# Hybrid decoder block on one core: a group's small matmuls gathered in two places, and a final norm by square root and one Newton step

## The chip, the cores and the metric

The kernel runs on one core of one Trainium2 chip. The metric is the device time of one execution in microseconds (us). Three timed runs of the kernel before gave 611.32, 611.39 and 611.45, median 611.39. One more execution was taken with the hardware profiler.

## The reference, cut to what matters

The input is 256 tokens of width 1024. One combined projection feeds a Mamba-2 mixer (A) and a causal attention (B); both are projected, merged by gates and added to the residual; a gated FFN with a short convolution follows, and a final RMS norm.

```
def hybrid_layer(x, ...):
    proj = rmsnorm(x, norm1_w) @ w_in
    z, xbc_raw, dt_raw, q, k, v, g_raw = split(proj)
    y_ssd = ssd_mixer(z, xbc_raw, dt_raw, ...)        # 32 heads of 64 in 8 groups, state 128, chunk 128
    y_att = moba_attention(rope(q), rope(k), v)       # 16 heads of 64; 256 tokens are one block: plain causal attention
    merged = g_ssd * (y_ssd @ w_ssd_proj) + g_att * (y_att @ w_att_proj)
    x = x + merged @ w_out
    a, gb = split(rmsnorm(x, norm2_w) @ w_ffn_up)     # 2 x 2816
    return x + (silu(causal_dwconv(a)) * gb) @ w_ffn_down
out = rmsnorm(hybrid_layer(x, ...), norm_f_w)         # rmsnorm(x) = x * rsqrt(mean(x*x) + 1e-6) * w
```

## The kernel before, in words

**Units of weights.** Weights stream in as units of up to 128 partitions x 8 x 256 numbers (1 MB), in the order of the list `seq` (L99 on), on SyncE's DMA queue. `next_unit` (L117) loads three units ahead and splits one unit ahead. A split (`split_unit`, L86) works by halves of 1024 columns: ScalarE writes `hi`, the rounded part in the fp32r type (L93), VectorE writes `lo`, the rest (L94). There are four buffers for `hi` and four for `lo`, so a half is split when the half two units earlier is done with. Each product is three TensorE matmuls: hi by hi, hi by lo, lo by hi. `mm_unit` (L129, lines L148 to L150) has the weights stationary and 256 tokens moving: 48 matmuls of 256 columns for a unit. `mm_tok` (L152, lines L165 to L167) has 128 tokens stationary and 512 weight columns moving: 24 matmuls of 512 columns.

**Groups.** The first half of the kernel is a loop over eight groups g (L544). Each group has the unit products `u_bc`, `u_x`, `u_qk`, `u_z` and, in odd groups, `u_v` (lines L327 to L329), in even groups two units of a gate (`u_gate`, in four quarters of a half unit each, driven as a generator). Between the units stand small matmuls in plain float32:

- `s_cb` (L342): C times B into `pcb` (L345, L346); VectorE masks it into `cb` (L348); ScalarE makes the decay matrices `mx` from `acsB` (L354 to L357); VectorE multiplies `mx` by `cb` (L359).
- `s_xt` (L361): four transposes into `pxt` (L366), and VectorE's `xt` (L368).
- `s_y` (L371): sixteen small products `py` of `mx` and `xt` (L381), then the gate by `zt` (L385, L386) and the squares.
- `s_st` (L390): the column sums `stat` (L200) and the reciprocal root on VectorE (`rms_rstd`, L176); `s_pb` (L393): its broadcast `pb` (L210), then `yn`.
- `a_s` (L402): attention scores `s_ps` (L410) and the softmax; `a_t` (L428): six transposes `pt_ps` (L433); `a_o` (L438): `po` (L447) and `yatt`.

In one group the order before is: `u_bc(g)`, `s_y(g-1)`, `u_x(g)`, `a_s(g-1)`, `u_qk(g)`, `s_cb(g)` with `s_st(g-1)`; then in odd groups `u_v`, `a_t(g-1)`, `u_z`, and `s_xt(g)`, `a_o(g-1)`, `s_pb(g-1)` together; in even groups `u_z`, `a_t(g-1)` with `s_xt(g)`, half of the gate, `a_o(g-1)` with `s_pb(g-1)`, the rest of the gate. So TensorE leaves the big products for small ones five times in a group. After the loop the last group's `s_y`, `a_s`, `s_st`, `a_t`, `s_pb`, `a_o` stand between the four units of the first SSD projection.

**PSUM.** Eight banks: three `mm`, two `at` (scores, transposes of the softmax), two `ss` (`pcb`, `pxt`, `stat`, `pb`), one `acc` (`py`, `po`).

**Who sets the order.** TensorE runs in the order of the program (`manual_schedule` over PE alone). For VectorE, ScalarE and the others a planner, with its own estimate of times, fixes an order beforehand; each engine then takes its instructions strictly in that order, so an instruction that waits holds up those behind it.

**The end.** The down projection (L727 on) runs two halves h of 512 output columns, each over 22 tiles k in units of 4, 4, 4, 4, 4 and 2 tiles; in the last unit, token half c = 0 comes first. For h = 1, VectorE adds the residual (L733), ScalarE squares and sums the row (L658), `rms_rstd` makes the reciprocal root by an integer guess (L183) and three Newton steps (L187, L191), and then ScalarE scales the first 512 columns (L740) and VectorE the last 512 (L742), each with its DMA to the output (L741, L743).

Of the kernel before, what the change touches and what calls it, by code (L numbers as in the profile page):

```python
# [8 lines left out]
F32 = mybir.dt.float32  # L9
# [29 lines left out]
def block_kernel(tc, xtok_d, par_d, nf_d, con_d, rope_d, wdt_d, win_d, wgate_d, bg_d, watt_d, wssd_d, wout_d, wup_d, wdn_d, out_d):  # L39
# [3 lines left out]
    with st:  # L43
# [66 lines left out]
        seq += [(wdn_d[h, :, b : min(b + 8, 2 * NF)], min(8, 2 * NF - b)) for h in range(2) for b in range(0, 2 * NF, 8)]  # L110
        raws, units = [], []

        def load_to(n):
# [35 lines left out]
                    nc.tensor.matmul(ps[m], wh, xl, start=False, stop=False)  # L149
                    nc.tensor.matmul(ps[m], wl, xh, start=False, stop=z)  # L150

        def mm_tok(ps, halves, act, k0, nk, by_token=False, cs=(0, 1)):  # L152


            kt = [(hi, lo, kk) for hi, lo, n in halves for kk in range(0, n, 2)]
            order = [(k, c) for k in range(len(kt)) for c in cs]
            if by_token:
                order.sort(key=lambda x: x[1])
            with tc.manual_schedule(engines=PE_ONLY):
                for k, c in order:  # L160
                    hi, lo, kk = kt[k]
                    wh, wl = (w[:, kk : kk + 2].rearrange("p a b -> p (a b)") for w in (hi, lo))
                    xh, xl = (act[k0 + k][:, i, c * P : c * P + P] for i in range(2))
                    o = ps[c].rearrange("p a b -> p (a b)")
                    nc.tensor.matmul(o, xh, wh, start=(k0 + k == 0), stop=False)  # L165
                    nc.tensor.matmul(o, xh, wl, start=False, stop=False)  # L166
                    nc.tensor.matmul(o, xl, wh, start=False, stop=(k0 + k == nk - 1))  # L167

        def mm_tile():
            return ps_mm.tile([P, 2, T], F32, tag="mm", bufs=3, name="mm")  # L170
# [21 lines left out]

        def rms_stat(sqs, inv_n):

            ps = ps_s.tile([P, 2, T], F32, tag="ss", bufs=2, name="stat")
            jobs = [(sq, ones[:, 0:1]) for sq in sqs]
            with tc.manual_schedule(engines=PE_ONLY):
                for i, (sq, one) in enumerate(jobs):
                    for c in range(2):
                        nc.tensor.matmul(ps[:, 0, c : c + 1], sq[:, c * P : c * P + P], one,  # L200
                                         start=(i == 0 and c == 0), stop=(i == len(jobs) - 1 and c == 1))
# [235 lines left out]

        def a_o(g):  # L438
            pts, vt = S[g]["pt"], S[g]["vt"]
            po = ps_s.tile([P, 2, T], F32, tag="acc", bufs=1, name="po")  # L440
            with tc.manual_schedule(engines=PE_ONLY):
                for c in range(2):
                    for j in range(2):
                        o = po[64 * j : 64 * j + 64, 0, :] if c == 0 else po[64 * j : 64 * j + 64, 0, P:T]
                        rhs = flat(pts[j][:, 0:2]) if c == 0 else pts[j][:, 2]
                        vc = (2 * (g % 2) + j) * 64
                        nc.tensor.matmul(o, vt[:, c, vc : vc + 64], rhs, start=(c == 0), stop=(c == 1))  # L447
            p = new_pair("yatt")
            split_pair(p, po[:, 0, :])
            yatt[g] = p  # L450
# [76 lines left out]
        def u_gate(j):  # L527
# [13 lines left out]
                nc.scalar.activation(gt, gt, AF.Tanh, scale=0.5)  # L541
            yield

        for g in range(NG):  # L544
            if g:
                u_bc(g)
                s_y(g - 1)
                u_x(g)
                a_s(g - 1)
            u_qk(g)  # L550
            if g == 0:
                for c in range(2):
# [12 lines left out]
            elif g % 2:  # L565
                s_cb(g)
                s_st(g - 1)
                u_v(g)
                a_t(g - 1)
                u_z(g)  # L570
                s_xt(g)
                a_o(g - 1)
                s_pb(g - 1)
            else:
                s_cb(g)
                s_st(g - 1)
                u_z(g)
                a_t(g - 1)
                s_xt(g)
                gate = u_gate(g // 2)  # L580
                next(gate)
                next(gate)
                a_o(g - 1)
                s_pb(g - 1)
# [12 lines left out]
        mm_tok(pss, next_unit(), yn, 8, 16)  # L597
        a_o(NG - 1)
        mm_tok(pss, next_unit(), yn, 12, 16, by_token=True)
        st_at.close()  # L600
        ssp_st.close()
# [49 lines left out]
                gated(t1, ps, c, 2 + h)  # L651
                nc.vector.tensor_tensor(m, t1, m, op=ALU.add)

        ss2, ss3 = (late.tile([P, 2, 2], F32, name=n) for n in ("ss2", "ss3"))

        def square_sum(dst, src):
            junk = late.tile([P, 512], F32, tag="junk", bufs=2, name="junk")
            nc.scalar.activation(junk, src, AF.Square, accum_out=dst)  # L658

        xw2 = [None] * KD  # L660

# [62 lines left out]
            act.append(p)  # L724

        rstd3 = late.tile([P, 2], F32, name="rstd3")
        for h in range(2):  # L727
            ps = [mm_tile(), mm_tile()]
            for k0 in range(0, NF, 4):
                mm_tok(ps, next_unit(), act, k0, NF, by_token=(k0 + 4 >= NF))  # L730
            for c in range(2):
                x = half(x2[:, c], h)
                nc.vector.tensor_tensor(x, ps[c].rearrange("p a b -> p (a b)"), x, op=ALU.add)  # L733
                square_sum(ss3[:, c, h : h + 1], x)
                if h == 0:
                    nc.gpsimd.tensor_tensor(x, x, half(nfb, 0), op=ALU.mult)
                else:
                    r = rstd3[:, c : c + 1]
                    rms_rstd(r, ss3[:, c, 0:1], 1.0 / D, more=ss3[:, c, 1:2])
                    nc.scalar.activation(half(x2[:, c], 0), half(x2[:, c], 0), AF.Identity, scale=r)  # L740
                    nc.scalar.dma_start(out_d[:, c, 0:512], half(x2[:, c], 0))  # L741
                    nc.vector.scalar_tensor_tensor(x, x, r, half(nfb, 1), op0=ALU.mult, op1=ALU.mult)  # L742
                    nc.sync.dma_start(out_d[:, c, 512:], x)  # L743


def _layout(i):
# [89 lines left out]
```

## Time and profile before

| | |
|---|---|
| median of three runs | 611.39 us |
| profiled execution: its time, and its span | 611.95 us, 610.1 us |
| TensorE busy with matmuls | 592.4 us |
| VectorE, ScalarE busy | 463.6 us, 358.4 us |
| the eight groups | about 14 to 321 us |
| projections, output projection, FFN up | about 321 to 544 us |
| FFN down and end | about 544 to 610 us |

Busy times are those of the whole span. A matmul's listed duration is its latency; matmuls overlap, so the pace of TensorE is read from the distance between two starts. In the rows of the time order the columns are start, duration, engine, line, operation, tiles and shape, how many are merged, and, in brackets, how long the engine stood idle before and what ended that.

### The profile page before, as it was taken

What the parts mean: (1) busy time and instruction counts of PE and PEld (TensorE: products, weight loads), DVE (VectorE), ACT (ScalarE), POOL (GpSimd) and SP (SyncE); (2) the same over time, 40 slices, a digit from 0 to 9 for tenths busy, and PEclk for the clock granted to TensorE, in tenths of its full rate; (3) what the DMA queues carried; (4) which work ended last, traced back from release to release, by engine and by line L of the source; (5) the groups of instructions that cost most, each with busy time, mean ns of one, the idle gap of its engine ahead of it and who ended that gap; (6) DMA issues with size and microseconds to landing.
All of it is one profiled execution on the core that took longest, in us unless ns stands there. A gap on an engine that the chain in (4) does not pass through costs nothing.

```text
span 610.1 us, 10606 instructions
## 1 busy us (share of the span) xinstructions
PE 592.4 (97%) x4194; PEld 543.0 (89%) x4194; DVE 463.6 (76%) x896; ACT 358.4 (59%) x648; POOL 4.1 (1%) x8
## 2 busy tenths in 40 slices
PE   7997999999999999999999999999999999999994
PEld 7996999989999899998988788889999999998883
DVE  5866798968979699796986546667988888884643
ACT  6646867649586495865945334456655555654431
POOL 0000000000000000000000000000000000000100
PEclk9999999999999999999999999999999999999998
DMA  8667265464534545445352755645446455455511
GB/s 330 228 250 271 102 212 173 156 218 136 195 138 172 210 151 182 138 162 208 122 197 102 260 202 192 206 153 193 162 185 205 155 193 196 160 198 179 200 35 69
DMA packets 17746, 109.78 MB, mean 180 GB/s; under 512 B 2176, under 2 KB 2592, under 8 KB 5664
## 3 DMA queue, kind: packets, MB, share of 16 engines
q1 hardware_dynamic: 15120, 100.15, 46.6%
q10 hardware_dynamic: 2576, 8.95, 4.3%
q8 instruction: 33, 0.54, 0.3%
q14 instruction: 17, 0.14, 0.1%
HBM read 107.49 MB, written 1.08 MB: 178 GB/s over the span
## 4 chain that ended last, share of the span: by engine, by line
PE 92%; ACT 3%; DMA 2%; DVE 2%; issue 1%; ACTq 0%; DVEq 0%
PE mm L148 16%; PE mm L149 16%; PE mm L150 16%; PE mm L165 11%; PE mm L167 10%; PE mm L166 10%; PE py L381 2%; PE mm L328 1%; PE mm L327 1%; PE mm L329 1%; DMA acsB<-acsT_d 1%; PE s_ps L410 1%; PE po L447 1%; PE pt_ps L433 1%; ACT hi L93 1%; PE pb L210 1%
## 5 line engine op out<-in xcount | busy, mean ns | idle before, releaser
L93 ACT ACTIVATE hi<-raw 128x1024 fp32r<-128x1024 f32 x186 | 196.0, 1060 | 179.3 <-PE mm L167 79.4
L94 DVE TENSOR_TENSOR lo<-raw,hi 128x1024 fp32r<-128x1024 f32 x186 | 226.7, 1226 | 89.3 <-ACT hi L93 89.0
L148 PE MATMUL mm<-hn,hi 128*128 128x256 f32 x512 | 147.4, 288 | 0.0
L149 PE MATMUL mm<-hn,hi 128*128 128x256 f32 x512 | 145.0, 283 | 0.4 <-DVE hn L220 0.4
L150 PE MATMUL mm<-hn,lo 128*128 128x256 f32 x512 | 144.8, 283 | 0.0
L148 PEld LDWEIGHTS mm<-hn,hi 128*128 128x128 f32 x512 | 98.0, 191 | 4.1 <-issue 3.9
L148 PE MATMUL mm<-xw,hi 128*128 128x256 f32 x352 | 99.8, 283 | 0.0
L149 PE MATMUL mm<-xw,hi 128*128 128x256 f32 x352 | 99.6, 283 | 0.0
L150 PE MATMUL mm<-xw,lo 128*128 128x256 f32 x352 | 99.6, 283 | 0.0
L149 PEld LDWEIGHTS mm<-hn,hi 128*128 128x128 f32 x512 | 98.2, 192 | 0.9 <-DVE hn L220 0.8
L150 PEld LDWEIGHTS mm<-hn,lo 128*128 128x128 f32 x512 | 98.1, 192 | 0.0
L149 PEld LDWEIGHTS mm<-xw,hi 128*128 128x128 f32 x352 | 67.6, 192 | 0.0
L148 PEld LDWEIGHTS mm<-xw,hi 128*128 128x128 f32 x352 | 67.6, 192 | 0.0
L150 PEld LDWEIGHTS mm<-xw,lo 128*128 128x128 f32 x352 | 67.6, 192 | 0.0
L272 DVE SCALAR_TENSOR_TENSOR cacc<-mm,par,cacc 128x255 f32<-128x255 f32 (+2 forms) x96 | 44.2, 475 | 3.0 <-ACT cacc L268 2.9
L165 PE MATMUL mm<-hi,act 128*128 128x512 f32 x88 | 34.2, 389 | 0.0
L166 PE MATMUL mm<-lo,act 128*128 128x512 f32 x88 | 34.2, 389 | 0.0
L167 PE MATMUL mm<-hi,act 128*128 128x512 f32 x88 | 34.2, 389 | 0.0
L166 PE MATMUL mm<-lo,hn 128*128 128x512 f32 x64 | 25.0, 391 | 1.7 <-DVE lo L94 1.7
L165 PE MATMUL mm<-hi,hn 128*128 128x512 f32 x64 | 25.8, 404 | 0.0
L165 PE MATMUL mm<-hi,yn 128*128 128x512 f32 x64 | 25.3, 396 | 0.0
L167 PE MATMUL mm<-hi,hn 128*128 128x512 f32 x64 | 25.0, 391 | 0.0
(170 smaller groups left out, 935.4 us busy)
## 6 DMA issues: line engine op xcount, KB each, us to landing
raw<-in_win_dram SPq DMA_DIRECT2D x35, 1024.0 KB
raw<-in_wup_dram SPq DMA_DIRECT2D x22, 1024.0 KB
raw<-in_wdn_dram SPq DMA_DIRECT2D x10, 1024.0 KB
raw<-in_wgate_dram SPq DMA_DIRECT2D x8, 1024.0 KB
raw<-in_wssd_dram SPq DMA_DIRECT2D x8, 1024.0 KB
acsB<-acsT_d ACTq DMA_DIRECT2D x8, 512.0 KB
raw<-in_watt_dram SPq DMA_DIRECT2D x4, 1024.0 KB
raw<-in_wout_dram SPq DMA_DIRECT2D x4, 1024.0 KB
```

Of the source, the lines that this page charges most:

```text
L93: nc.scalar.activation(hi[:, :n], raw[:, k0 : k0 + n], AF.Copy)
L94: nc.vector.tensor_tensor(lo[:, :n], raw[:, k0 : k0 + n], hi[:, :n].bitcast(F32), op=ALU.subtract)
L148: nc.tensor.matmul(ps[m], wh, xh, start=a, stop=False)
L149: nc.tensor.matmul(ps[m], wh, xl, start=False, stop=False)
L150: nc.tensor.matmul(ps[m], wl, xh, start=False, stop=z)
L165: nc.tensor.matmul(o, xh, wh, start=(k0 + k == 0), stop=False)
L166: nc.tensor.matmul(o, xh, wl, start=False, stop=False)
L167: nc.tensor.matmul(o, xl, wh, start=False, stop=(k0 + k == nk - 1))
L210: nc.tensor.matmul(pb[:, 0, c * P : c * P + P], y[:, c : c + 1].to_broadcast([P, P]), ident, start=True, stop=True)
L272: nc.vector.scalar_tensor_tensor(acc[:, s:], src[:, m, : T - s], w(m, 3 - s), acc[:, s:], op0=ALU.mult, op1=ALU.add)
L327: nc.tensor.matmul(ps[:, c, :], xh, hi[:, kk], start=(k == 0 and c == 0), stop=False)
L381: nc.tensor.matmul(o, xt[:, c, r, :], rhs, start=(c == 0), stop=(c == 1))
```

## The change

Three things are edited.

First, the small matmuls of a group stand in two places, and the end of the attention (`a_o`, with `s_pb`) a group and a half behind its group's units. `small_1(g)` comes after `u_x(g)`: `s_y(g-1)`, `a_s(g-1)`, `a_o(g-2)`, `s_pb(g-2)`. `small_2(g)` comes after the last unit of an odd group and after the third quarter of the gate in an even group: `s_cb(g)`, `s_xt(g)`, `s_st(g-1)`, `a_t(g-1)`. `stat` and `po` swap their PSUM banks. After the loop `small_1(8)` follows `small_2(7)` with no unit between.

Second, the final norm of token half c takes a square root on ScalarE, a reciprocal and one Newton step on VectorE, and a `Sqrt` of one column is put after the last FFN activation.

Third, in the down projection the units become 2, 4, 4, 4, 4, 4 tiles; in the last unit of h = 1, token half 0 is finished first, and token half 1 in two pieces of 256 columns, each added and squared by itself. This end is issued in program order on TensorE, ScalarE and VectorE.

```diff
+IN_ORDER = {mybir.EngineType.PE, mybir.EngineType.Activation, mybir.EngineType.DVE}
...
+        DOWN = ((0, 2), (2, 6), (6, 10), (10, 14), (14, 18), (18, 22))
...
-            ps = ps_s.tile([P, 2, T], F32, tag="ss", bufs=2, name="stat")
+            ps = ps_s.tile([P, 2, T], F32, tag="acc", bufs=1, name="stat")
...
-            po = ps_s.tile([P, 2, T], F32, tag="acc", bufs=1, name="po")
+            po = ps_s.tile([P, 2, T], F32, tag="ss", bufs=2, name="po")
...
+        def small_1(g):
+            if 0 <= g - 1 < NG:
+                s_y(g - 1)
+                a_s(g - 1)
+            if 0 <= g - 2:
+                a_o(g - 2)
+                s_pb(g - 2)
+
+        def small_2(g):
+            if g < NG:
+                s_cb(g)
+                s_xt(g)
+            if 0 <= g - 1:
+                s_st(g - 1)
+                a_t(g - 1)
...
                 u_bc(g)
-                s_y(g - 1)
                 u_x(g)
-                a_s(g - 1)
+                small_1(g)
             u_qk(g)
...
-                s_cb(g)
-                next(gate)
-                s_xt(g)
                 next(gate)
                 next(gate)
+                small_2(g)
+                next(gate)
             elif g % 2:
-                s_cb(g)
-                s_st(g - 1)
                 u_v(g)
-                a_t(g - 1)
                 u_z(g)
-                s_xt(g)
-                a_o(g - 1)
-                s_pb(g - 1)
+                small_2(g)
...
-        s_y(NG - 1)
-        a_s(NG - 1)
+        small_1(NG)
         pss = [mm_tile(), mm_tile()]
         mm_tok(pss, next_unit(), yn, 0, 16)
-        s_st(NG - 1)
+        small_2(NG)
         mm_tok(pss, next_unit(), yn, 4, 16)
-        a_t(NG - 1)
         s_pb(NG - 1)
+        a_o(NG - 1)
         mm_tok(pss, next_unit(), yn, 8, 16)
-        a_o(NG - 1)
         mm_tok(pss, next_unit(), yn, 12, 16, by_token=True)
...
+        nc.scalar.activation(root[:, 0:1], th[:, 0:1], AF.Sqrt, scale=0.0, bias=eps)
...
+        def root3(c, n):
+            nc.scalar.activation(root[:, c : c + 1], ss3[:, c, n - 1 : n], AF.Sqrt, scale=1.0 / D, bias=fin[:, c, 0:1])
+
+        def rstd_3(c, n):
+
+            mh, h, r = (fin[:, c, i : i + 1] for i in (1, 2, 3))
+            nc.vector.scalar_tensor_tensor(h, ss3[:, c, n - 1 : n], -0.5 / D, mh, op0=ALU.mult, op1=ALU.add)
+            nc.vector.reciprocal(r, root[:, c : c + 1])
+            nc.vector.scalar_tensor_tensor(h, r, r, h, op0=ALU.mult, op1=ALU.mult)
+            nc.vector.scalar_tensor_tensor(rstd3[:, c : c + 1], h, 1.5, r, op0=ALU.add, op1=ALU.mult)
...
+        with tc.manual_schedule(engines=IN_ORDER):
+            for a in (0, 256):
+                mm_tok(ps, hv, act, k0, NF, cs=(1,), cols=slice(a, a + 256))
+            mean3(0, 2)
+            add_x3(ps, 1, 0)
+            root3(0, 2)
+            add_x3(ps, 1, 1, 0, 0, 256)
+            rstd_3(0, 2)
+            out_lo(0)
+            mean3(1, 3)
+            add_x3(ps, 1, 1, 1, 256, 512)
+            root3(1, 3)
+            out_hi(0)
+            rstd_3(1, 3)
+            out_lo(1)
+            out_hi(1)
```

`mean3` makes the part of the mean square that is known before the last piece (two to four operations on one column); `add_x3` adds the residual on VectorE and squares and sums on ScalarE; `out_lo` scales on ScalarE and issues the output's DMA on ScalarE's queue; `out_hi` scales on VectorE and issues on SyncE's.

More of the change, by code (lines that the diff above doesn't have):

```diff
@@ L109, in block_kernel @@
         seq += [(wup_d[f], KD) for f in range(NF)]
[L110 removed]
+        DOWN = ((0, 2), (2, 6), (6, 10), (10, 14), (14, 18), (18, 22))
+        seq += [(wdn_d[h, :, 2 * a : 2 * b], 2 * (b - a)) for h in range(2) for a, b in DOWN]
         raws, units = [], []
@@ L161, in mm_tok @@
                     hi, lo, kk = kt[k]
-                    wh, wl = (w[:, kk : kk + 2].rearrange("p a b -> p (a b)") for w in (hi, lo))
+                    wh, wl = (w[:, kk : kk + 2].rearrange("p a b -> p (a b)")[:, cols] for w in (hi, lo))
                     xh, xl = (act[k0 + k][:, i, c * P : c * P + P] for i in range(2))
-                    o = ps[c].rearrange("p a b -> p (a b)")
+                    o = ps[c].rearrange("p a b -> p (a b)")[:, cols]
                     nc.tensor.matmul(o, xh, wh, start=(k0 + k == 0), stop=False)
                     nc.tensor.matmul(o, xh, wl, start=False, stop=False)
-                    nc.tensor.matmul(o, xl, wh, start=False, stop=(k0 + k == nk - 1))
+                    nc.tensor.matmul(o, xl, wh, start=False, stop=(k0 + k == nk - 1 and cols.stop == 512))
         def mm_tile():
@@ L582, in block_kernel @@
                 next(gate)
-                a_o(g - 1)
-                s_pb(g - 1)
+                small_2(g)
                 next(gate)
@@ L652, in block_kernel @@
                 nc.vector.tensor_tensor(m, t1, m, op=ALU.add)
-        ss2, ss3 = (late.tile([P, 2, 2], F32, name=n) for n in ("ss2", "ss3"))
+        ss2 = late.tile([P, 2, 2], F32, name="ss2")
         def square_sum(dst, src):
             junk = late.tile([P, 512], F32, tag="junk", bufs=2, name="junk")
-            nc.scalar.activation(junk, src, AF.Square, accum_out=dst)
+            nc.scalar.activation(junk[:, : src.shape[1]], src, AF.Square, accum_out=dst)
         xw2 = [None] * KD
@@ L726, in block_kernel, with add_x3 @@
         rstd3 = late.tile([P, 2], F32, name="rstd3")
+        ss3 = late.tile([P, 2, 4], F32, name="ss3")
+        eps = late.tile([P, 1], F32, name="eps")
+        nc.vector.memset(eps, EPS)
+        root = late.tile([P, 2], F32, name="root")
+        nc.scalar.activation(root[:, 0:1], th[:, 0:1], AF.Sqrt, scale=0.0, bias=eps)
+        def add_x3(ps, h, c, i=0, a=0, b=512):
+            x = half(x2[:, c], h)[:, a:b]
+            nc.vector.tensor_tensor(x, flat(ps[c])[:, a:b], x, op=ALU.add)
+            square_sum(ss3[:, c, h + i : h + i + 1], x)
@@ new lines, in block_kernel, with mean3 @@
+        fin = late.tile([P, 2, 4], F32, name="fin")
+        def mean3(c, n):
+            m, mh = fin[:, c, 0:1], fin[:, c, 1:2]
+            nc.vector.tensor_scalar(m, ss3[:, c, 0:1], 1.0 / D, EPS, op0=ALU.mult, op1=ALU.add)
+            for i in range(1, n - 1):
+                nc.vector.scalar_tensor_tensor(m, ss3[:, c, i : i + 1], 1.0 / D, m, op0=ALU.mult, op1=ALU.add)
+            nc.vector.tensor_scalar(mh, m, -0.5, None, op0=ALU.mult)
+        def root3(c, n):
+            nc.scalar.activation(root[:, c : c + 1], ss3[:, c, n - 1 : n], AF.Sqrt, scale=1.0 / D, bias=fin[:, c, 0:1])
@@ new lines, in rstd_3, with out_lo @@
+        def rstd_3(c, n):
[4 more added lines that the diff above has]
+            nc.vector.scalar_tensor_tensor(rstd3[:, c : c + 1], h, 1.5, r, op0=ALU.add, op1=ALU.mult)
+        def out_lo(c):
+            x = half(x2[:, c], 0)
+            nc.scalar.activation(x, x, AF.Identity, scale=rstd3[:, c : c + 1])
+            nc.scalar.dma_start(out_d[:, c, 0:512], x)
@@ L727, in block_kernel, with out_hi @@
+        def out_hi(c):
+            x = half(x2[:, c], 1)
+            nc.vector.scalar_tensor_tensor(x, x, rstd3[:, c : c + 1], half(nfb, 1), op0=ALU.mult, op1=ALU.mult)
+            nc.sync.dma_start(out_d[:, c, 512:], x)
         for h in range(2):
             ps = [mm_tile(), mm_tile()]
[L729 to L735, printed above, removed]
-                    nc.gpsimd.tensor_tensor(x, x, half(nfb, 0), op=ALU.mult)
[L737 to L743, printed above, removed]
@@ new lines, in block_kernel @@
+            for k0, _ in DOWN[:-1]:
+                mm_tok(ps, next_unit(), act, k0, NF)
+            hv, k0 = next_unit(), DOWN[-1][0]
+            mm_tok(ps, hv, act, k0, NF, cs=(0,))
+            if h == 0:
+                add_x3(ps, h, 0)
+                mm_tok(ps, hv, act, k0, NF, cs=(1,))
+                add_x3(ps, h, 1)
+                for c in range(2):
+                    x = half(x2[:, c], 0)
+                    nc.gpsimd.tensor_tensor(x, x, half(nfb, 0), op=ALU.mult)
+        with tc.manual_schedule(engines=IN_ORDER):
[14 more added lines that the diff above has]
+            out_hi(1)
```

6 lines of the change are left out of this document (1 added, 5 removed).

## The prediction

> **What bounds the kernel now.** I read the page first, then the stretches, then TensorE's waits.
>
> ```profile
> span 610.1 us, 10606 instructions
> PE 592.4 (97%) x4194; PEld 543.0 (89%) x4194; DVE 463.6 (76%) x896; ACT 358.4 (59%) x648; POOL 4.1 (1%) x8
> ```
>
> ```profile
> 212.20:287.60 75.40, 75.40 (x589) 70.13 (x588) 63.16 (x136) 52.60 (x107) 0.00 (x0) 1.00 0.50 169
> 603.00:610.10 7.10, 0.00 (x0) 0.00 (x0) 2.93 (x15) 1.44 (x2) 0.00 (x0) 0.64 0.39 149
> ```
>
> ```profile
> PE mm L166 <- DVE lo L94: 1.7, 1, 1.7
> PE py L381 <- DVE mx L359: 1.7, 1, 1.7
> PE py L381 <- DVE yatt L174: 1.4, 1, 1.4
> ```
>
> The stretches have, after their bounds and length, the busy time of TensorE, its weight loads, VectorE, ScalarE and GpSimd, the granted clock, the DMA share and GB/s; the waits have their total, number and longest. TensorE is the bound: in two middle groups (75.40 us) it is busy all the time at full clock, VectorE 84% of it. Time can come out in three ways: fewer seams in TensorE's stream, the three waits above (4.8 us in all), and the end after the last matmul. A gain under 0.2% of 611.4, which is 1.2 us, could not be told from no change.
>
> **Part 1: the seams.** The distance between starts is what an instruction costs TensorE.
>
> ```profile
> 136.50 0.28 PE L149 MATMUL mm<-hn,hi 128*128 128x256 f32 x1
> 136.62 0.28 PE L150 MATMUL mm<-hn,lo 128*128 128x256 f32 x1
> 136.83 1.52 PE L381 MATMUL py<-mx,xt 128*64 128x256 f32 x16
> 138.28 0.39 PE L148 MATMUL mm<-hn,hi 128*128 128x256 f32 x1
> 138.50 0.28 PE L149 MATMUL mm<-hn,hi 128*128 128x256 f32 x1
> ...
> 150.94 0.59 PE L345 MATMUL pcb<-bc 128*128 128x256 f32 x2
> ...
> 151.59 0.50 PE L200 MATMUL stat<-ones,zt 128*128 128x1 f32 x4
> 151.96 0.36 PE L327 MATMUL mm<-hi,hn 128*128 128x256 f32 x1
> 152.16 0.28 PE L328 MATMUL mm<-lo,hn 128*128 128x256 f32 x1
> ```
>
> A 256-column matmul follows another after 0.12 us (136.50 to 136.62), so a unit of 48 takes 5.76. Into `py`, which fills half the array, the step is 0.21, and out of it the first big matmul takes 0.22 instead of 0.12: 0.19 lost. Out of `stat` it is 0.20: 0.08 lost. The whole price in a group comes from the chain of waits:
>
> ```profile
> 212.31 1.45 PE py L381 x16
> 247.40 1.45 PE py L381 x16
> ```
>
> From `py` to `py` through an odd group are 35.09 us; five units are 28.80; so the small matmuls with their seams cost 6.29. What they cost back to back is seen at the end of the loop, where they stand together already:
>
> ```profile
> 315.02 0.60 PE L366 MATMUL pxt<-con,xs 128*128 128x128 f32 x4
> 315.54 0.87 PE L447 MATMUL po<-pt,vt 128*64 128x256 f32 x8
> 316.35 0.71 PE L210 MATMUL pb<-con,ry 128*128 128x128 f32 x4
> 318.46 1.52 PE L381 MATMUL py<-mx,xt 128*64 128x256 f32 x16 [1.41 <-DVE yatt L174]
> 319.91 0.93 PE L410 MATMUL s_ps<-qk 64*128 64x128 f32 x8
> 320.77 0.50 PE L165 MATMUL mm<-hi,yn 128*128 128x512 f32 x1
> ...
> 332.25 0.82 PE L433 MATMUL pt_ps<-con,pr 128*128 128x128 f32 x6
> 332.91 0.61 PE L210 MATMUL pb<-con,ry 128*128 128x128 f32 x4
> 333.27 0.48 PE L165 MATMUL mm<-hi,yn 128*128 128x512 f32 x1
> ```
>
> First place: entry 0.09, `py` 1.45, `s_ps` 0.86, `po` 0.81, `pb` 0.36, exit 0.08 to 0.10: 3.66. Second place: `pcb` 0.65, `pxt` 0.44 to 0.52 (0.52 holds an entry into `po`), `stat` 0.37, `pt_ps` up to 0.66, exit 0.08: 2.1 to 2.3. Together 5.8 to 5.9 against 6.29: 0.35 to 0.5 saved in a group. The loop has seven such groups: 2.5 to 3.5. At worst the switch from one kind of small matmul to the next costs as much as a seam, and nothing is saved. I take **-3.2**, since each piece has its own row.
>
> **Part 2: the two waits of the first groups.**
>
> ```profile
> 46.13 0.69 DVE L368 TENSOR_TENSOR xt<-pxt,dt 128x512 f32<-128x512 f32 x1 [1.91 <-PE pxt L366]
> 46.74 4.62 DVE L94 TENSOR_TENSOR lo<-raw,hi 128x1024 fp32r<-128x1024 f32 x4
> ...
> 59.11 1.76 DVE L359 TENSOR_TENSOR mx<-mx,cb 128x1536 f32<-128x1536 f32 x1 [2.68 <-ACT mx L357]
> ```
>
> In the first group VectorE stood idle for `pxt` with four `lo` queued behind `xt`, and TensorE missed the first: 1.7. Now `pxt` comes a quarter of the gate later, behind the matmuls that need this `lo`, so `lo` must come first. The other wait: `py(0)` stood for the `mx` product, which ended at 60.87. `py(0)` now has `u_x(1)`, 5.76 us, ahead of it; 1.7 goes, and the `mx` product, bound by a DMA and ScalarE, is late no more. Next late would be the second `lo` of the gate's last quarter, behind `xt` as before. Between 0 and -3.4; I take **-2.5**.
>
> **Part 3: the end of the loop.** `small_1(8)` follows `small_2(7)` directly, so `py(7)` needs what has just been started. From the start of `pcb`, VectorE must wait some 0.85 (estimate: `pcb` 0.65 and a hand-over), then `cb` (about 0.55, three quarters of the 0.69 of `xt`), `mx` 1.76 and `xt` 0.69: 3.7 at best, with a `lo` of 1.16 and the gate's `zt` (0.69 as `xt`) ahead, 5.5. TensorE has 2.2 us of work until then. It waits 1.5 to 3.3, where it now stands 1.75 (318.46 less 316.35 and 0.36). So -0.2 to +1.6; I take **+0.8**.
>
> **Part 4: the end.**
>
> ```profile
> 600.72 0.39 PE L166 MATMUL mm<-lo,act 128*128 128x512 f32 x1
> 600.94 0.39 PE L167 MATMUL mm<-hi,act 128*128 128x512 f32 x1
> 601.37 0.69 DVE L733 TENSOR_TENSOR x<-mm,x 128x512 f32<-128x512 f32 x1 [0.67 <-PE mm L167]
> 602.09 0.63 ACT L658 ACTIVATE junk<-x 128x512 f32<-128x512 f32 x1 [0.64 <-DVE x L733]
> 602.63 0.19 ACT L658 ACTIVATION_READ_ACCUMULATOR junk<-x 128x1 f32 x1
> 604.87 0.22 DVE L187 SCALAR_TENSOR_TENSOR ra<-rstd,rh 128x1 f32<-128x1 f32 x1
> 605.12 0.16 DVE L191 SCALAR_TENSOR_TENSOR rstd<-ra,rstd 128x1 f32<-128x1 f32 x1
> 605.38 0.72 ACT L740 ACTIVATE x<-x,rstd 128x512 f32<-128x512 f32 x1 [0.84 <-DVE rstd L191]
> 606.13 0.36 ACTq L741 DMA_DIRECT2D out_dram<-x  x1
> ```
>
> From the last add (601.37) to the last scaling (605.38) are 4.01 us: add and square 1.45, the rest the integer guess and Newton chain, each pair of steps about 0.45. Afterwards the last piece is 256 columns. Counted from TensorE's end: VectorE is held about 0.2 by the first token half's root steps; the add takes about 0.42 (between half and all of 0.69); ScalarE is free at 0.84, because `out_lo(0)` with its 0.72 and the DMA issue's 0.36 stand ahead of the square in program order; square and read about 0.52; the one-column root 0.2 to 0.4 (between the read of 0.19 and the 0.63 square), taken 0.3; then reciprocal and two steps at 0.2 to 0.25 each: scaling starts at about 2.4. That saves 1.6. Against it TensorE's last unit: 24 matmuls at 0.12 are 2.88, where twelve at 0.22 to 0.23 take 2.72: +0.16. The output DMA behind it stays. Ends: -2.0 if ScalarE is not held, -0.7 if the dependent steps cost double. I take **-1.4**.
>
> **The cover of part 1.** It is a saving only if nobody comes too late in the new order. The tightest distance is now two units (11.5 us): from `pcb` to the next `py`, and from `stat` to its `pb`. In between VectorE owes `cb` (0.55), the `mx` product (1.76), `xt` (0.69) and the root's dozen steps of 0.2 to 0.25, some 5.7 us, beside four `lo` of 1.16. It fits, and `hi` and `lo` run a unit ahead. The new bank neighbours (`stat` behind `py`, `po` behind `pcb` and `pxt`) were read two units earlier. Taken at nothing; without that cover it is the first rival.
>
> **The table.** The `Sqrt` needs another one. The trace shows one load:
>
> ```profile
> 0.73 1.28 ACT L66 ACT_TABLE_LOAD   x1 [0.73 <-PEq L824]
> ```
>
> A second of 1.28 would come as the down projection starts; ScalarE is idle for 41% of the span and runs a unit ahead: hidden, and 1.28 if not. The Trainium skill (ScalarE: Activation LUTs, section "What ACT_TABLE_LOAD costs") gives 1283 ns, as the row has, and adds a drain of 1380 ns to each switch, which no row here shows; by 2.66 us it would be hidden too.
>
> **Sum.** -3.2 - 2.5 + 0.8 - 1.4 = -6.3. The profiled execution took 611.95 (span 610.1 and 1.85 around it): 605.65. It lay 0.56 above the median of the runs, so **605.1**.
>
> **The rivals.**
>
> *A new convoy on VectorE (slower).* The small places now hand VectorE four things at once. The row at 46.13 shows what happens when the planner puts one that must wait ahead of `lo`: 1.7 us of TensorE. If `py`'s readers or `xt` do that once in each of seven groups, 11.9 come on top: 617.0. From 0.9 us per group the gain of 6.3 is gone. For it: VectorE is 84% busy. Against it: TensorE waits nowhere for over 0.2 us between 62 and 315 us with the same work and the same planner. 10%.
>
> *The first groups wait as before*, `xt` merely blocking another `lo`, and `py(0)` waiting because ScalarE is given `mx` later: 607.6. The planner's estimates failed there once already. 16%.
>
> *The seams are not saved*: each change of kind inside a place costs as much as a seam, so part 1 does not do what it says: 608.3. Against it the back-to-back rows. 12%.
>
> *The tables alternate in the end.* If `Square` and `Sqrt` did not share a table, three loads of 1.28 would fall between the squares and the roots on ScalarE's path, some of the first hidden: about +3.4, 608.5. The Trainium skill (same page, "Table sets: the hidden batching unit") says to batch by set and names relu, copy, identity and abs as common to all sets, not square, which would give just this. 4%.
>
> *Two of the last three together*: about 611. 4%.
>
> **How the numbers follow.** The forecast has 54%. Faster: the forecast and the three middle rivals, 86%; within 0.2%: 4%; slower: 10%. The range goes from 602.8 (parts 2 and 4 near their best ends) to 609.0 (the fourth rival and a little), and leaves out the convoy and the pairs.
>
> **What would show it.** TensorE should leave the big products twice in a group; from `py` to `py` in an odd group should be about 34.6 instead of 35.09; the waits at 48 and 61 us should be gone; at the loop's end one wait of 1.5 to 3.3 before `py`; from TensorE's end to the last scaling about 2.4; two table loads, the second as the down projection starts. New waits of TensorE on `lo` or `mx` between 62 and 310 us, more than two loads, or a distance of 35 or more from `py` to `py` would prove me wrong.

## The result, and the profile after

The changed kernel is slower: median 618.93 us (618.07 to 620.94), beside 611.36 for the kernel before on the same chip; the ratio is 1.0121, with a 95% interval of 1.0102 to 1.0139. The forecast was 605.1, within 602.8 to 609.0. The profiled execution took 618.93 us, its span 617.1. (The ratio is not taken from the two medians and can differ a little from their quotient.)

The page of the changed kernel, with the busy times and the granted clock in forty slices:

```profile
span 617.1 us, 10666 instructions
PE 596.1 (97%) x4206; PEld 549.1 (89%) x4206; DVE 461.9 (75%) x891; ACT 359.3 (58%) x654; POOL 3.9 (1%) x8
PEclk8999989999999999999988999999999999999998
```

VectorE and ScalarE have about as much to do as before (461.9 and 359.3 us busy, where it was 463.6 and 358.4). What is new is in the clock row: it falls at the start, in the sixth slice (77 to 93 us) and in the two slices from 309 to 339 us. The waits of TensorE name the later places, one for the sixth slice and two for the pair:

```profile
PE mm L330 <- DVE lo L95: 3.7, 1, 3.7
PE py L383 <- DVE rv L182: 3.1, 1, 3.1
PE pb L212 <- DVE ry L193: 2.0, 1, 2.0
```

The three waits of before (1.7, 1.7, 1.4) are gone but for 0.3, and these three of 8.8 us have come. To see where the 7.0 us of span lie, both runs are cut at the same matmuls: the first small matmul behind the units of group 1, the one behind the units of group 7, the broadcast of the second norm's factor as the FFN begins, the end. First the kernel before, then the changed one (bounds, length, then busy time of TensorE, its weight loads, VectorE, ScalarE and GpSimd, then granted clock, DMA share, GB/s):

```profile
0.00:88.80 88.80, 81.24 (x629) 75.75 (x630) 66.15 (x150) 55.92 (x109) 1.19 (x6) 1.00 0.64 232
88.80:315.02 226.22, 226.22 (x1767) 210.41 (x1766) 190.20 (x409) 157.56 (x321) 0.00 (x0) 1.00 0.49 170
315.02:422.79 107.77, 106.36 (x553) 88.97 (x552) 70.18 (x120) 52.32 (x81) 0.00 (x0) 1.00 0.54 186
422.79:610.10 187.31, 178.54 (x1254) 167.90 (x1252) 137.09 (x218) 92.60 (x137) 2.92 (x2) 0.99 0.47 163
```

```profile
0.00:90.03 90.03, 82.70 (x615) 77.42 (x615) 62.98 (x136) 55.29 (x107) 1.19 (x6) 0.96 0.63 231
90.03:313.59 223.56, 223.56 (x1767) 210.03 (x1765) 186.33 (x406) 155.64 (x321) 0.00 (x0) 1.00 0.48 169
313.59:429.82 116.23, 111.09 (x567) 92.97 (x565) 76.38 (x139) 53.22 (x83) 0.00 (x0) 0.97 0.52 177
429.82:617.10 187.28, 178.69 (x1266) 168.64 (x1264) 136.25 (x212) 95.14 (x143) 2.75 (x2) 0.99 0.47 163
```

The six middle groups, the body of the change, are 2.66 us shorter, 0.44 a group. The end is as long as before. The loss stands in the first and the third stretch. `pcb`, `stat` and `pt_ps` of one group with their seams (0.65, 0.37, 0.66 and 0.08, together 1.76 us) stood ahead of both cuts and now stand behind them, so they have moved from the first stretch to the third; with that, the first stretch has lost 3.0 and the third 6.7. Of the 3.0, 1.48 lie at the very start: TensorE's clock is at half from 8.6 to 12.0 us, and the first `ps_dt` starts at 20.37 instead of 18.89. That is not the change's doing: of three kernels below that have the loop of before unchanged, the profiles of two show this window and that of the third does not. So 1.5, -2.7, 6.7 and 0 are to be explained.

**The first groups.** ScalarE, then VectorE, then TensorE of the changed kernel, in order of time:

```profile
49.84 0.35 ACTq L301 DMA_DIRECT2D acsB<-acsT_d  x1
...
57.45 0.69 ACT L356 ACTIVATE mx<-acsB,acs 128x128 f32<-128x128 f32 x2 [2.75 <-DMA acsB<-acsT_d]
```

```profile
54.73 1.23 DVE L95 TENSOR_TENSOR lo<-raw,hi 128x1024 fp32r<-128x1024 f32 x1 [0.40 <-ACT hi L94]
62.05 1.76 DVE L361 TENSOR_TENSOR mx<-mx,cb 128x1536 f32<-128x1536 f32 x1 [6.10 <-ACT mx L359]
...
75.89 1.22 DVE L95 TENSOR_TENSOR lo<-raw,hi 128x1024 fp32r<-128x1024 f32 x1
```

```profile
77.17 0.58 PE L330 MATMUL mm<-lo,hn 128*128 128x256 f32 x1 [3.70 <-DVE lo L95]
77.55 0.41 PE L331 MATMUL mm<-hi,hn 128*128 128x256 f32 x1
...
80.32 0.28 PE L329 MATMUL mm<-hi,hn 128*128 128x256 f32 x1
80.44 0.28 PE L330 MATMUL mm<-lo,hn 128*128 128x256 f32 x1
```

The load of `acsB(0)` takes 7.6 us from its issue. ScalarE has the decay matrices of group 0 at the head of its order and waits for it; VectorE has their product at the head of its order and stands idle for 6.10. Everything behind, the convolution of group 1 and the splits, comes late, and `u_v(1)` is the unit that finds no `lo`: 3.7 us. Then, up to 80.32, the steps are 0.21 instead of 0.12: half clock, 1.5 us more (3.15 us for 14 steps of 0.12).

**The end of the loop.** TensorE, then VectorE:

```profile
313.59 0.59 PE L347 MATMUL pcb<-bc 128*128 128x256 f32 x2
...
315.04 0.85 PE L435 MATMUL pt_ps<-con,pr 128*128 128x128 f32 x6
319.01 2.65 PE L383 MATMUL py<-mx,xt 128*64 128x256 f32 x16 [3.12 <-DVE rv L182]
...
325.83 1.04 PE L212 MATMUL pb<-con,ry 128*128 128x128 f32 x4 [2.02 <-DVE ry L193]
327.09 0.63 PE L168 MATMUL mm<-lo,yn 128*128 128x512 f32 x1
328.37 0.63 PE L168 MATMUL mm<-lo,yn 128*128 128x512 f32 x1
```

```profile
313.13 0.69 DVE L317 TENSOR_TENSOR swap<-swap,rope 128x512 f32<-128x512 f32 x1 [1.65 <-DMA swap<-qkraw]
...
316.53 1.75 DVE L361 TENSOR_TENSOR mx<-mx,cb 128x1536 f32<-128x1536 f32 x1
318.20 0.69 DVE L370 TENSOR_TENSOR xt<-pxt,dt 128x512 f32<-128x512 f32 x1
318.80 0.15 DVE L182 TENSOR_SCALAR rv<-stat 128x2 f32<-128x2 f32 x1
...
325.62 0.16 DVE L193 SCALAR_TENSOR_TENSOR ry<-ra,ry 128x2 f32<-128x2 f32 x1
```

`py(7)` needs `mx`, `xt` and the bank from which `rv` reads `stat`; VectorE has them one behind the other, after a swap that waited 1.65 for its DMA, so the wait is called `rv` but is the queue ahead of it. `pb(6)` waits again, for a root chain whose dozen steps VectorE has mixed with splits and softmax: `stat` stands at 314.68, `ry` at 325.62. `py` takes 2.65 instead of 1.52, and between the last two rows three matmuls take 1.28 instead of 0.68: half clock. The visit costs 13.07 us (the distance between the big matmuls around it, less their own step), where a pair of visits in the middle costs 5.89.

**The end.**

```profile
608.23 0.28 PE L169 MATMUL mm<-hi,act 128*128 128x256 f32 x1
608.55 0.42 DVE L742 TENSOR_TENSOR x<-mm,x 128x256 f32<-128x256 f32 x1 [2.18 <-PE mm L169]
...
612.38 0.72 ACT L768 ACTIVATE x<-x,rstd 128x512 f32<-128x512 f32 x1 [0.74 <-DVE rstd L764]
```

The addition of the first piece could start some 1.4 us before TensorE's end; it starts 0.04 after it. From TensorE's end (608.51) to the last scaling are 3.87 us; before they were 4.05 (601.33 to 605.38).

**The theories.** Mine: three separate places, each to be mended by itself, while the middle of the loop brings what was forecast. The rival: an overload of VectorE, or the clock, that shows in these places by chance and would turn up elsewhere.

### The profile page after: what moved, and what is told of

It is laid out like the page before. It is cut to its first block, busy times and chain, and to the rows that moved or that the text cites. A ratio compares the mean times of both kernels' runs of the same rounds, so it can differ in the third digit from the quotient of the medians.

```text
span 617.1 us, 10666 instructions
## 1 busy us (share of the span) xinstructions
PE 596.1 (97%) x4206; PEld 549.1 (89%) x4206; DVE 461.9 (75%) x891; ACT 359.3 (58%) x654; POOL 3.9 (1%) x8
## 4 chain that ended last, share of the span: by engine, by line
PE 87%; ACT 5%; DVE 3%; DMA 3%; issue 1%; ACTq 0%; DVEq 0%
PE mm L151 15%; PE mm L150 15%; PE mm L152 15%; PE mm L168 10%; PE mm L167 10%; PE mm L169 10%; PE py L383 2%; ACT hi L94 1%; DMA acsB<-acsT_d 1%; PE mm L330 1%; PE mm L331 1%; ACT mx L356 1%; PE mm L329 1%; PE s_ps L412 1%; PE pb L212 1%
## 5 line engine op out<-in xcount | busy, mean ns | idle before, releaser
L274 DVE SCALAR_TENSOR_TENSOR cacc<-mm,par,cacc 128x253 f32<-128x253 f32 (+2 forms) x96 | 44.3, 477 | 2.1 <-ACT cacc L270 1.6
L168 PE MATMUL mm<-lo,act 128*128 128x512 f32 (+1 forms) x92 | 35.0, 380 | 0.0
L167 PE MATMUL mm<-hi,act 128*128 128x512 f32 (+1 forms) x92 | 34.9, 380 | 0.0
L169 PE MATMUL mm<-hi,act 128*128 128x512 f32 (+1 forms) x92 | 34.9, 380 | 0.0
L167 PE MATMUL mm<-hi,yn 128*128 128x512 f32 x64 | 25.9, 404 | 0.0
L167 PE MATMUL mm<-hi,hn 128*128 128x512 f32 x64 | 25.5, 399 | 0.0
L168 PE MATMUL mm<-lo,yn 128*128 128x512 f32 x64 | 25.4, 397 | 0.0
L169 PE MATMUL mm<-hi,yn 128*128 128x512 f32 x64 | 25.4, 397 | 0.0
```

The source lines that it names most:

```text
L274: nc.vector.scalar_tensor_tensor(acc[:, s:], src[:, m, : T - s], w(m, 3 - s), acc[:, s:], op0=ALU.mult, op1=ALU.add)
```

## The experiments

Each is compared with runs of the kernel before on the same chip (611.37 to 611.40).

### The new end alone

The kernel before, with only the second and third edit of the change (the diff's core stands in the section on the change).

```diff
+        DOWN = ((0, 2), (2, 6), (6, 10), (10, 14), (14, 18), (18, 22))
...
+        nc.scalar.activation(root[:, 0:1], th[:, 0:1], AF.Sqrt, scale=0.0, bias=eps)
...
+            for a in (0, 256):
+                mm_tok(ps, hv, act, k0, NF, cs=(1,), cols=slice(a, a + 256))
```

> The kernel before with the new end alone: its loop, the places of its small matmuls and its buffers are as they were; only the final rms by square root and one Newton step, the sums by halves and the outputs' order are changed. Theory A (three separate places: the two calls that meet at the end of the loop, the first group's late decay product, and an end whose first half is let go only with the second): the new end gives nothing by itself, 611.4 us within 0.5, and from TensorE's last product to the end of the last scaling it takes about 3.9 us, as in the changed kernel (3.87). Theory B (the new end itself is dear, by a table load or by its longer chain): 613 us or more, and the rest of the loss would then lie in it. The prediction's own figure for the end would give 610.0.

Measured: 610.99 us, ratio 0.9997 (0.9986 to 1.0007); 3.87 us from TensorE's last product (602.49) to the last scaling (606.36). The new end costs nothing and brings nothing that can be told from zero. Its table is loaded behind the last FFN activation (in the changed kernel at 555.39, the second of two loads), and TensorE waits for nothing there.

### The two calls apart

```diff
                 u_v(g)
+                if g == NG - 1:
+                    small_2(g)
                 u_z(g)
-                small_2(g)
+                if g < NG - 1:
+                    small_2(g)
```

> The changed kernel, but in the last group the second call of the small matmuls stands behind the unit of v and ahead of the unit of z, so that the unit of z (about 14 us) lies between it and the next first call. Theory A: the waits of 3.1 us (for rv) and 2.0 us (for ry) at the loop's end go or fall under 0.5 us together, and the half-speed windows behind them with them: 5 to 6.7 us less than the changed kernel, 612.2 to 613.9 us. Theory B (VectorE is loaded too evenly in every group, and the end of the loop only shows what has piled up; or the clock alone): the waits turn up elsewhere, and it stays above 616.9 us.

Measured: 613.02 us, ratio 1.0033 (1.0017 to 1.0049): 5.9 us less than the changed kernel. TensorE:

```profile
315.98 1.52 PE L383 MATMUL py<-mx,xt 128*64 128x256 f32 x16
...
321.40 0.71 PE L212 MATMUL pb<-con,ry 128*128 128x128 f32 x4 [2.25 <-DVE ry L193]
```

The wait before `py` is gone, and no half-clock window is left here. The wait at `pb` stays, which the theory had not expected: from `stat` (309.08) to `pb` are only one unit and the calls' own matmuls, and the root chain needs more.

### The last piece whole

```diff
-            for a in (0, 256):
-                mm_tok(ps, hv, act, k0, NF, cs=(1,), cols=slice(a, a + 256))
+            mm_tok(ps, hv, act, k0, NF, cs=(1,))
...
-            add_x3(ps, 1, 1, 0, 0, 256)
...
-            add_x3(ps, 1, 1, 1, 256, 512)
+            add_x3(ps, 1, 1)
```

> The changed kernel, but the second half of the tokens in the last unit goes in one piece of 512 columns instead of two pieces of 256, its addition, squares, root and Newton step too; the first half's scaling and output stand between. Theory A (the first piece of 256 was released no earlier than the second, so cutting bought nothing and cost 0.16 us on TensorE and two more links on VectorE): from TensorE's last product to the end of the last scaling about 2.6 us instead of 3.87, and 617.5 us in all, 1.4 less than the changed kernel. Theory B (the end is set by the outputs' transfers, or by the table): no change within 0.4 us, 618.5 to 619.3.

Measured: 616.43 us, ratio 1.0075 (1.0054 to 1.0096), 2.5 us less. From TensorE's last product (607.68) to the last scaling (610.45) are 2.77 us, 1.1 less than in two pieces. The rest is mainly the clock (cut as above, the profile is 1.25 us shorter in the last stretch, 2.5 shorter at the loop's end and 1.8 longer in the first groups), and this makes the run worth more than it was meant for. Its loop is that of the changed kernel, and the waits at the loop's end are as long:

```profile
320.74 1.52 PE L383 MATMUL py<-mx,xt 128*64 128x256 f32 x16 [3.03 <-DVE rv L182]
...
326.76 0.71 PE L212 MATMUL pb<-con,ry 128*128 128x128 f32 x4 [2.85 <-DVE ry L193]
...
327.54 0.40 PE L168 MATMUL mm<-lo,yn 128*128 128x512 f32 x1
327.77 0.39 PE L169 MATMUL mm<-hi,yn 128*128 128x512 f32 x1
```

But here the clock stays full behind them (at 77 us its half-speed window is twice as long instead): `py` in 1.52, steps of 0.23 behind. The visit costs 11.91, which is 5.88 of waits and 6.03 of work; the changed kernel's 13.07 are 5.14 of waits, 5.89 of work and 2.0 of half clock, with another 1.1 in the unit behind. So the waits are the larger part and the half clock follows them or not.

### The decay product behind the convolution

`s_cb(0)` without its activations and product, which are called behind `u_bc(1)` and held there in the order of both engines:

```diff
+            if g:
+                s_mx(g)
...
                 u_bc(g)
+                if g == 1:
+                    s_mx(0)
+                    load_acs(1)
```

> The changed kernel, but the decay product of group 0 (twelve activations, the common exponential and VectorE's product) is called behind the unit of B and C of group 1 and held there in the order of ScalarE and VectorE, so that the three splits and the convolutions of group 1 stand ahead of it while it waits for its transfer. Theory A: the 3.7 us wait for lo at about 77 us and the half-speed window behind it go: 3.7 to 5 us less than the changed kernel, 613.9 to 615.2 us, unless the product is then late for its own reader (py of group 0, about 90 us), which would give a wait of 1 us or more there. Theory B (the wait at 77 us comes from too much work on VectorE ahead of it, not from the transfer): a wait of 3 us or more remains before the matmuls of v, and the time stays within 1 us of 618.9.

Measured: 623.6 us, ratio 1.0191 (1.0167 to 1.0216), 4.7 more. The wait for `lo` went, as expected, and the wait that had been named as a reservation came, at eight times the size. VectorE and TensorE:

```profile
71.53 1.76 DVE L370 TENSOR_TENSOR mx<-mx,cb 128x1536 f32<-128x1536 f32 x1 [3.64 <-ACT mx L368]
```

```profile
73.34 2.83 PE L394 MATMUL py<-mx,xt 128*64 128x256 f32 x16 [8.03 <-DVE mx L370]
```

A queue in strict order has one head: putting the late thing behind the others makes it later by all of them. The order was not the fault to mend; the lateness was.

### The broadcast earlier

```diff
+                dt_turn()
+                load_acs(0)
                 gate = u_gate(0)
                 next(gate)
-                dt_turn()
-                load_acs(0)
```

> The changed kernel, but the turn of the running sums and the load of group 0's broadcast (acsB) stand ahead of the first quarter of the gate unit instead of behind it. In the run with the decay product behind the convolution the wait for lo went and a wait of 8.0 us for the product came, so the order of the two only chooses which one is late. Theory A (both are late because the broadcast lands late): landing about 4 us earlier, the product is done before the splits need the engines, the wait at 77 us (3.7 to 4.3 us in three runs) falls under 1 us with no wait for the product in its place, less up to 1 us of a new wait of TensorE for the running sums at 40 us: 613.9 to 616 us. Theory B (ScalarE and VectorE have too much work there, whatever the transfer does): a wait of 3 us or more stays in u_v or comes at py, and the time stays above 617.5 us.

Measured: 613.79 us, ratio 1.0034 (1.0021 to 1.0047), 5.1 less. ScalarE, then VectorE:

```profile
54.16 0.70 ACT L356 ACTIVATE mx<-acsB,acs 128x128 f32<-128x128 f32 x2 [3.31 <-DMA acsB<-acsT_d]
```

```profile
66.58 1.21 DVE L95 TENSOR_TENSOR lo<-raw,hi 128x1024 fp32r<-128x1024 f32 x1
```

The split that `u_v(1)` needs starts at 66.58 instead of 75.89, and TensorE waits 0.76 for another `lo` at 62 us and 0.32 for the running sums at 39 us. The broadcast itself lands 3.3 us earlier, of which 1.5 is the start's clock window, absent here. That window is not what mended the place: the run with the calls apart is without it too, has its broadcast only at 56.52 and waits 4.2 us for `lo`. Against that run the broadcast lands 2.4 us earlier, though its issue is at 48.39 in both; beside that the planner put one more split ahead of the convolution. How much is the one and how much the other was not tried apart. Of the 5.1 us some 1.5 are the start's window: from the first `ps_dt` to the cut behind group 1 the trace is 3.8 shorter (65.89 instead of 69.66).

### All three

The edits of the calls apart, the last piece whole and the earlier broadcast in one kernel:

```diff
+                if g == NG - 1:
+                    small_2(g)
                 u_z(g)
...
+                dt_turn()
+                load_acs(0)
                 gate = u_gate(0)
...
+            mm_tok(ps, hv, act, k0, NF, cs=(1,))
```

> The three edits in one kernel: the second call ahead of the unit of z in the last group, the last unit's second token half in one piece, and the early turn of the running sums. Theory A (three separate places): the gains add up, 618.93 less 5.9 (measured), less 1.1 to 2.5 (measured; 1.1 in the trace's end), less 3 to 5: 606 to 609 us, which beats the kernel before (611.4) too. Theory B (the first place doesn't move): 610 to 612 us.

Measured: 606.48 us, ratio 0.9919 (0.9904 to 0.9934). The three gains measured singly make 13.5 us, together 12.45. These sums are not clean, since the start's half-clock window is in the profile of the changed kernel and not in those of the calls apart, the earlier broadcast and this kernel. Cut at the same matmuls, this trace is 3.8 us shorter from the first `ps_dt` to the cut behind group 1 (the earlier broadcast alone: 3.8), 6.1 shorter from there to the FFN (the calls apart alone: 6.2) and 1.2 shorter in the last stretch (the piece whole alone: 1.25). These 11.1 add up as three separate places do; another 1.45 are the start's window. This kernel beats both.

### The broadcast of the root's factor one unit later

On the kernel with all three edits:

```diff
-        small_1(NG)
+        s_y(NG - 1)
+        a_s(NG - 1)
+        a_o(NG - 2)
         pss = [mm_tile(), mm_tile()]
         mm_tok(pss, next_unit(), yn, 0, 16)
+        s_pb(NG - 2)
         small_2(NG)
```

> As the kernel with all three edits, and the broadcast of the rms factor for group 6 (s_pb, four small matmuls) stands behind the first unit of the token projection instead of inside the first call. In the run with the calls apart TensorE still waited 2.2 us for ry at that place. Theory A (that wait is only distance: the root chain has 8 us from its sums, behind lo and the softmax on VectorE): it goes, 1.5 to 2.3 us less than with the three edits. Theory B (VectorE is so full at the loop's end that whatever stands last is late): the wait comes back at the next reader, within 0.6 us of the three edits.

Measured: 605.80 us, ratio 0.9903 (0.9890 to 0.9916), 0.7 less than with the three edits, between the two forecasts; the single runs of the two kernels overlap (605.36 to 606.13 and 605.81 to 608.32), so the gain is small beside their spread. The 2.37 us wait at `pb` is gone; waits of 0.39 (`pt_ps` for ScalarE's softmax) and 0.44 (the next `pb`) came. The three visits behind the loop cost 7.83 where they cost 8.70.

### The kernel before, with the last piece whole

The first kernel of this list with the edit of the third:

```diff
-            for a in (0, 256):
-                mm_tok(ps, hv, act, k0, NF, cs=(1,), cols=slice(a, a + 256))
+            mm_tok(ps, hv, act, k0, NF, cs=(1,))
```

> The kernel before with the new end, the second token half of the last unit in one piece of 512 columns: its loop is as before. The end alone, in two pieces, gave 610.99 (3.87 us from TensorE's last product to the last scaling, 4.05 in the kernel before). Theory A: 2.8 us from TensorE's end to the last scaling, as in the changed kernel with one piece (2.77), and 609.6 to 610.1 us. Theory B (the end is bound otherwise, by the transfers out): 610.8 to 611.2.

Measured: 609.72 us, ratio 0.9976 (0.9966 to 0.9986); from TensorE's last product (600.88) to the last scaling (603.66) 2.78 us. With the piece whole, the new end is worth 1.65 us beside the kernel before, and 1.27 beside the two pieces.

### Two pieces in two tiles

```diff
+            psb = mm_tile()
+            mm_tok(ps, hv, act, k0, NF, cs=(1,), cols=slice(0, 256))
+            mm_tok([None, psb], hv, act, k0, NF, cs=(1,), cols=slice(256, 512), own=True)
...
+            nc.vector.tensor_tensor(x, flat(ps[1]), x, op=ALU.add)
+            square_sum(ss3[:, 1, 1:2], x[:, 0:256])
...
+            add_x3([None, psb], 1, 1, 1, 256, 512)
```

(`own` starts a sum of its own in the second tile; the loop of pieces and their two additions go.)

> The kernel before with the new end in two pieces, as measured alone (610.99), but the last unit's second piece of 256 columns is summed in a tile of its own and added by itself; the first piece's tile is then complete when the first piece is. The first addition is of 512 columns. Theory A (the end gained nothing because both pieces stand in one tile, which is let go with its last product): the first addition starts about 1.4 us before TensorE's end, and from TensorE's last product to the last scaling it takes 2.4 to 2.7 us instead of 3.87: 609.5 to 609.9 us, about as with one piece (609.72). Theory B (VectorE's chain of small operations for the first token half holds the second addition): 3.4 us or more, above 610.6 us.

Measured: median 610.53 us, ratio 0.9977 (0.9962 to 0.9992). In time order:

```profile
601.20 0.69 DVE L795 TENSOR_TENSOR x<-mm,x 128x512 f32<-128x512 f32 x1 [0.74 <-PE mm L169]
...
602.32 0.28 PE L169 MATMUL mm<-hi,act 128*128 128x256 f32 x1
...
605.30 0.72 ACT L766 ACTIVATE x<-x,rstd 128x512 f32<-128x512 f32 x1 [0.74 <-DVE rstd L762]
```

The first addition starts 1.4 us before TensorE's end (602.60), and the last scaling comes 2.70 behind it. So what held it was that both pieces were one sum in one tile, and not VectorE's chain of small operations. (The tile and the end mark `stop`, which the first piece's last product has only here, were not tried apart.) The profiled execution (611.40) has the start's half-clock window. Two others took as long, at the same granted clock of 0.994 on record; the other three took 609.63 to 609.76 at 0.996 to 0.998, as with the piece whole.

### The calls meet in the middle of the loop

On the kernel of 605.80:

```diff
                 u_x(g)
-                small_1(g)
+                if g != 4:
+                    small_1(g)
...
                     small_2(g)
+                if g == 3:
+                    small_1(g + 1)
```

> The kernel with the three edits and s_pb behind (605.8), but now the two calls meet in the middle of the loop: the first call of group 4 stands directly behind the second call of group 3, ahead of the units of B, C and x of group 4, as the two stood at the loop's end in the changed kernel. Theory A (two calls that meet cost TensorE the length of the chains between them, wherever they stand): waits of about 3 us for rv or mx at py and about 2 us for ry at pb, 5.1 to 6.7 us more, 610.9 to 612.5 us. Theory B (only the loop's end is tight, as the attention's last softmax and the missing weights come together there): less than 2 us more.

Measured: 614.97 us, ratio 1.0048 (1.0031 to 1.0065): 9.2 more than without. TensorE:

```profile
164.32 2.83 PE L383 MATMUL py<-mx,xt 128*64 128x256 f32 x16 [2.84 <-DVE rv L182]
...
171.79 0.71 PE L212 MATMUL pb<-con,ry 128*128 128x128 f32 x4 [2.90 <-DVE ry L193]
```

The same two waits, in the same places, of about the same size: two calls that meet cost this much in the middle of the loop as well. The size was underrated: the visit costs 13.16 us, 7.3 more than a pair, but the runs lie between 613.14 and 616.13. The profiled one, 613.14, is the shortest and has one window of half clock besides the end. The three longest (615.57 to 616.13) have a granted clock of 0.989 on record, the profiled one 0.994; over 614 us that is some 3 us of full clock less (an estimate from these figures). So the clock can account for most of what the 9.2 has beyond the 7.3; where it fell is not known, as these runs were not profiled.

## Why the prediction was wrong

**Where the error lies.** The span grew by 7.0 us, where the sum said -6.3. Of these 13.3, 5.9 lie at the loop's end, 4.0 in the first groups, 1.5 in the half clock at the very start, 1.4 in the end, and 0.5 in part 1 (-2.7 for the six middle groups, -3.2 forecast for seven).

**Part 1 (-3.2) was right.** From `py` to `py` in an odd group:

```profile
218.14 1.52 PE L383 MATMUL py<-mx,xt 128*64 128x256 f32 x16
...
252.81 1.52 PE L383 MATMUL py<-mx,xt 128*64 128x256 f32 x16
```

34.67 us, forecast "about 34.6"; a pair of visits costs 5.89, forecast 5.8 to 5.9, and TensorE is busy without a gap in six groups. Costing the small matmuls from a place where they already stood back to back gave the right price. (In groups 2, 4 and 6 `small_2` stands behind half of the gate; behind its third quarter, as said of all even groups, it stands in group 0 alone. The tightest distance is that of the odd groups either way.)

**The cover of part 1, "taken at nothing", is the step that failed.** It named the tightest distance, "two units (11.5 us)", and found the chains to fit. That holds in every group but two. At the loop's end the distance from `pcb` to `py` and from `stat` to `pb` is no unit at all, and part 3 asked this only of `py`. Its price there was near: a wait of 1.5 to 3.3 was forecast, 3.12 came. What it left out is `pb(6)`, whose `ry` starts from the `stat` of the same visit: 2.0 to 2.85 us in the changed kernel and the three runs above that keep the two calls together at this place; and the clock, about 3 us in the profiled run. Instead of +0.8 the stretch cost +6.7, and the runs with the calls apart and with the calls met in group 4 show that the meeting is the cause.

**Part 2 (-2.5) was half right.** Both old waits went, as said. "Next late would be the second `lo` of the gate's last quarter" was wrong: the next late thing was the decay product itself, held by its DMA, and behind it everything on two engines up to `u_v(1)`, 20 us after the load had landed. "The `mx` product, bound by a DMA and ScalarE, is late no more" looked at the reader of `mx` and not at what is queued behind `mx`. Net +1.5 instead of -2.5; with the broadcast earlier, the old waits and this one are gone, but for 0.76 and 0.32 us at two other places.

**Part 4 (-1.4) failed on one assumption,** that the first piece could be added while the second ran. Both stand in one tile, whose release comes with its last product, so VectorE had both additions and the first half's root steps behind TensorE's end. With two tiles the forecast's 2.4 measured 2.70, with the piece whole 2.78. The table load was hidden, as said.

**The rivals.** The convoy on VectorE is the rival that came, 10% in the forecast and 617.0 us. But its mechanism was one stall in each of seven groups; it came in two places only, each larger. The number is near for another reason. The seams, the tables and the first groups "as before" did not come.

**The sum.** With the three places mended, and `pb` a unit later, the kernel takes 605.80, 0.7 from the forecast of 605.1. That is another kernel than the one forecast, so its time does not bear the forecast out; but its trace, cut as above and with the moved matmuls allowed for, shows the gains that were counted: 2.3 us less than before in the first groups, 2.9 from there to the FFN and 1.2 in the end. What was missing was a look at the two places where the regular pattern of the loop does not hold.

## What to carry to other kernels

A new order of a loop should be laid out instruction by instruction at its first and its last turn, where neighbours meet that never meet in the middle, and for every chain that crosses the edge, not the first one only. When something waits at the head of a queue in strict order, mend its lateness; moving it behind the others only changes who waits. Cutting a sum into pieces helps only if the pieces are released apart.

## What the hardware showed that was not expected

The half clock comes in windows of 3.41 us (or twice that) on the trace's record. Within one execution they all start on one grid: in the changed kernel at 8.62, 76.89, 319.24 and 326.06 us, which are 20, 71 and 2 steps of 3.413 us apart, and by whole steps in every other profile with more than one. So a wait does not start a window by itself; what goes with a window, in all these profiles, is how little TensorE was busy in the step of the grid just before. Two steps of the changed kernel, then two of the run with the last piece whole, at the waits of the loop's end (columns as in the stretches above):

```profile
315.83:319.24 3.41, 0.29 (x3) 0.20 (x4) 3.41 (x6) 0.65 (x2) 0.00 (x0) 1.00 0.91 308
322.65:326.06 3.41, 1.39 (x14) 0.71 (x11) 3.07 (x20) 1.56 (x5) 0.00 (x0) 1.00 0.68 271
```

```profile
318.91:322.32 3.41, 1.58 (x18) 1.12 (x20) 3.41 (x7) 0.00 (x0) 0.00 (x0) 1.00 0.56 235
322.32:325.74 3.42, 1.60 (x16) 0.88 (x16) 3.42 (x18) 1.01 (x2) 0.00 (x0) 1.00 0.48 125
```

Behind the first two the clock was halved, behind the last two it was not. In the twelve profiles every step at full clock in which TensorE was busy for 1.49 us or less was followed by half clock, and none with 1.67 us or more was; of four with 1.58 to 1.60 us, one was. A window went on for a second step where TensorE was busy for 2.56 us or less in the first, and ended where it was busy for 2.96 us or more. (Busy time is that of the listed durations, so these bounds hold for this way of counting.)

This is why waits of 3.7, 4.2, 4.3 and 8.0 us were each followed by a window and shorter ones were followed by one or not: 3.12 and 2.02 us brought two windows, 2.84 and 2.90 us with the calls met in group 4 one, 3.03 and 2.85 us with the piece whole none. The grid lies differently against the kernel in each execution, so a part of these times is luck. The Trainium skill (TensorE: Matmul & The Clock Gate, section "What's actually happening") gives a window of 3413 ns that runs freely. The traces agree, in its length and in the grid. The same page of the Trainium skill (section "Why this matters for your kernels") advises against idle gaps of more than about 3 us; here a wait of 2.02 us with small matmuls around it was enough.
